# First unit loads, norm weights and tables issued from ScalarE in order of use, and five products of zeros between two feed forwards

## The chip, the cores and the metric

The kernel runs on one core of a Trainium2 chip. TensorE (PE) multiplies matrices, VectorE (DVE), ScalarE (ACT) and GpSimd (POOL) work element by element, and SyncE (SP) issues transfers between HBM and the core's memory; ScalarE and GpSimd can issue transfers too, as instructions in their own streams. The metric is the device time of one execution in microseconds, the median of three runs: 1272.45 us before the change (1271.78 to 1274.7).

## The reference

A block of two layers over 256 tokens of width 1024. Each layer adds half a gated feed forward, a mixer of three attentions, and half a second feed forward to the stream, every one behind a norm of its own; a last norm follows.

```python
def rms_norm(x, gain):
    xf = x.astype(jnp.float32)
    y = xf * lax.rsqrt(jnp.mean(xf * xf, axis=-1, keepdims=True) + NORM_EPS)
    return (y * gain.astype(jnp.float32)).astype(x.dtype)

def swiglu(h, w_gate, w_up, w_down):
    a = jnp.einsum('bsd,df->bsf', h, w_gate)
    u = jnp.einsum('bsd,df->bsf', h, w_up)
    return jnp.einsum('bsf,fd->bsd', jax.nn.silu(a) * u, w_down)
...
    for l in range(DEPTH):
        x = x + 0.5 * swiglu(rms_norm(x, ffn1_norm[l]), ffn1_w_gate[l], ffn1_w_up[l], ffn1_w_down[l])
        x = x + hybrid_mixer(rms_norm(x, mix_norm[l]), w_in[l], q_norm[l], w_uq[l], kv_norm[l], w_ukv[l],
                             w_br_mla[l], w_br_moba[l], w_br_dil[l], w_out[l])
        x = x + 0.5 * swiglu(rms_norm(x, ffn2_norm[l]), ffn2_w_gate[l], ffn2_w_up[l], ffn2_w_down[l])
    return rms_norm(x, final_norm)
```

The feed forward is 2816 wide, all weights are in 32 bits, and every weight is read from HBM once.

## The kernel before

**Products.** Every 32-bit product is made of three (`mm3`, L173): each operand is split into a high part, which ScalarE copies (`high`, L185), and a low part, which VectorE gets by subtraction (`low`, L188). So each block of weights passes through a load, a split on ScalarE and a low part on VectorE before TensorE may use it.

**A feed forward.** The 22 column blocks of 128 of the hidden layer come in three kinds. The first two are made row tile by row tile (`first_block`, L574), with b00 and b01 the gate and up sums of the first and the second 128 tokens; each goes through a silu on ScalarE (L564), a product on VectorE (L568, giving b00_h and b01_h) and transposes on TensorE (b0tp0, b0tp1). Eight single blocks follow (`block`, g2, u2, g3, u3 and so on). The last twelve are two units, each with a gate (G) and an up (U) matrix, made by Strassen's seven products in the order P1, P5, P6, P3, P7, P2, P4. Single blocks and the down products stand between those.

**A unit's quarters.** The weights of a unit's product come as quarters of 128 x 1536 (768 KB), kept in raw buffers a (two), b, c and d (one each). P1 loads a quarter into a, P5 one into b, P6 one into c, P2 one into d; the text calls the first unit's loads G1, G5, G6, G2, and the up matrix's first U1. P5 is made of a + b: VectorE adds G5 into G1 (L351), ScalarE splits the sum. P6 adds G6. GpSimd sends two further quarters that are added in memory while they are loaded.

**Order.** On TensorE, ScalarE and VectorE the instructions stand in the order in which the program writes them. Python plays through the products, counts their time in `clock`, and calls what was deferred (`defer`) when its time has come. Loads are called by `load_some` at a pace; a load's transfer is issued, and the first piece of its split follows at once (`until(total - 1)` in `load`). SyncE is not in that list: its stream holds transfers alone, each waits only for its buffer, so it runs ahead of the other engines until a slot is taken. Split weights lie in a ring of 6656 columns, raw ones in a ring of 4608.

**The start.** SyncE sends x, the first block's weights, then G1, rot and tab (`opened`, tables for the mixer), and only then waits for a slot. Nine products of zeros run first (L1186), while nothing has arrived.

**The norms.** `norm` (L405) is called by the stage before: squares on ScalarE (L429), the sum on VectorE (L435), the root on GpSimd (L436), the scaled rows on VectorE (L452), and `turn` transposes them on TensorE, half a row tile at a time. The weight row is fetched by `gain_tile` (L208) when the first half is done.

Of the kernel before, what the change touches and what calls it, by code (L numbers as in the profile page):

```python
# [110 lines left out]
def block_kernel(ctx: ExitStack, tc: tile.TileContext, a: dict, c: dict, out: bass.AP):  # L111
# [30 lines left out]
    def half_cols(h):  # L142
        return slice(h * 512, (h + 1) * 512)
# [25 lines left out]
    def transpose(o, src, n=P):  # L169
        nc.tensor.transpose(o, src, ident[:n, :n])  # L170
        spend(0.11)

    def mm3(o, st, mv, first, last, again=False):  # L173

        (sh, sl), (mh, ml) = st, mv
        nc.tensor.matmul(o, sh, mh, start=first, stop=False, skip_group_check=again)  # L176
        nc.tensor.matmul(o, sl, mh, start=False, stop=False, skip_group_check=again)  # L177
        nc.tensor.matmul(o, sh, ml, start=False, stop=last, skip_group_check=again)  # L178
        spend(3 * (max(256, o.shape[-1]) / 2400 + 0.003))
        load_some()  # L180
        while later and later[0][0] <= clock[0]:
            heapq.heappop(later)[2]()
# [25 lines left out]
    def gain_tile(src, n, name, tag):  # L208

        g = small.tile([P, n], F32, tag=tag, name=name, bufs=1)  # L210
        nc.sync.dma_start(g, bass.AP(tensor=src.tensor, offset=src.offset, ap=[[0, P], [1, n]]))
        return g

    def x_in(t):
# [98 lines left out]
    def load(j, ring):  # L313
        job = jobs[j]
        name, n = job["name"], job["n"]
        adds = []
        if "unit" in job:
            places, new, add, source, more = job["unit"]
            if new:
                tag, src = new  # L320
                places[tag] = raw_place("raw" + tag, unit_pool[0], 2 if tag == "a" else 1, [P, 4 * UC], f"{name}_r", j)
                nc.sync.dma_start(places[tag][0].rearrange("p (k n) -> p k n", k=4), src)
            for t in {source, *(add or ()), *(more or ())[:1]}:
                for i in places[t][1]:
                    if i in loaded:
                        loaded[i][2]()
                if places[t][1][-1] != j:
                    places[t][1].append(j)
            if more:
                tag, src = more  # L330
                nc.gpsimd.dma_start(places[tag][0].rearrange("p (k n) -> p k n", k=4), src, accum_op=ALU.add)
            raw = places[source][0]
            if add:
                to, other = [places[t][0] for t in add]
                adds = [(to, other)]
        else:
            o, old = take(raws, n, j)
            for i in old:
                loaded[i][2]()
            raw = raws["tile"][:, o:o + n]  # L340
            o = 0
            for w, k0, k1, c0, m in job["runs"]:
                e = o + (k1 - k0) * m
                nc.sync.dma_start(raw[:, o:e].rearrange("p (k n) -> p k n", k=k1 - k0),
                                  w[k0 * P:k1 * P, c0:c0 + m].rearrange("(k p) n -> p k n", p=P))
                o = e
        o, _ = take(rings[ring], n, j)
        hi, lo = [rings[ring][i][:, o:o + n] for i in ("hi", "lo")]
        piece = n // 2 if adds else n if job["whole"] else PIECE
        cuts = [(o, min(n, o + piece)) for o in range(0, n, piece)]  # L350
        todo = [lambda o=o, e=e: nc.vector.tensor_tensor(to[:, o:e], to[:, o:e], other[:, o:e], op=ALU.add)  # L351
                for to, other in adds for o, e in cuts]
        todo += [lambda o=o, e=e: high(hi[:, o:e], raw[:, o:e]) for o, e in cuts]
        todo += [lambda o=o, e=e: low(lo[:, o:e], raw[:, o:e], hi[:, o:e]) for o, e in cuts]
        total = len(todo)

        def until(m):
            while len(todo) > m:
                todo.pop(0)()

        size = piece / 1200 + 0.1
        for m in range(total - 1, -1, -1):
            defer(size * (total - 1 - m), lambda m=m: until(m))
        until(total - 1)
        loaded[j] = hi, lo, lambda: until(0), ring
        return SUM if adds else SPLIT if "unit" in job else PACE * n
# [35 lines left out]
        tl = const.tile([P, KT, S], F32R, tag="xTl", name=f"{name}_Tl")  # L402
        return th, tl

    def norm(name, gain_src, last=None, gain_cols=None):  # L405


        st = {}

        def half_done(t, h):  # L410
            if "g" not in st:
                g = gain_cols is None and gain_tile(gain_src, D, f"{name}_g", "gain")
                st["g"] = g and [g[:, half_cols(i)] for i in range(2)]
                if last is None:
                    nT[name] = transposed(name)
            if h == 0:
                if last is not None:
                    st["xg", t] = row_tile(f"{name}_xg{t}")
                if last is not None and t == 0:
                    st["sq"] = row_tile(f"{name}_sq")  # L420
                st[t] = st["sq"] if last is not None else row_tile(f"{name}_xs{t}"), small.tile([P, 2], F32, tag="ss", name=f"{name}_ss{t}"), \
                    small.tile([P, 1], F32, tag="rstd", name=f"{name}_r{t}")
            defer(0.7, lambda: square(t, h))
            if last is not None:
                nc.vector.tensor_tensor(st["xg", t][:, half_cols(h)], x[t][:, half_cols(h)], st["g"][h], op=ALU.mult)
# [28 lines left out]
            made.add((name, t, "rows"))  # L454

        def turn(t, h):
            tp = tp_bank(f"{name}_tp{t}{h}")
            for k in range(4):
                kk = h * 4 + k
                transpose(tp[:, k, :], st[t][0][:, kk * P:(kk + 1) * P])  # L460
            defer(0.3, lambda: parts_of(t, h, tp))
# [69 lines left out]
    def ffn(name, done, opening=None, opened=None):  # L531
        xTh, xTl = nT[name]
        steps, tail, f_first = ffn_steps()
        with ExitStack() as ctx2:
# [39 lines left out]
            def first_block():  # L574

                pair = hidden(0, 2)
                for t in range(NT):
# [17 lines left out]
                                            made.update((name, "hT", i, t) for i in range(2))))  # L595

                    glu(ab[:, 0, :], ab[:, 1, :], f"{name}_b0{t}", lambda h, t=t: defer(2.5, lambda: turn(t, h)), (name, "h", 0, t))
                if opening:
                    opened()

            single = {}

# [120 lines left out]

            first_block()
            for step in steps:
                if step[0] == "P":
                    unit_product(*step[1:])
                elif step[0] == "B":
                    block(*step[1:])
                else:  # L730
                    for t in range(NT):
                        for h in range(2):
                            down(step[1], t, h)
# [447 lines left out]
    nc.scalar.dma_start(gain_rows, a["ffn1_norm"][0].rearrange("(k p) -> k p", p=P))  # L1181
    nc.scalar.dma_start(ident, c["eye"])
    table(AF.Square)
    heat = acc_bank("heat")
    for _ in range(WARM):
        nc.tensor.matmul(heat[:, :256], zeros[:, :P], zeros, start=True, stop=True)  # L1186
    gain_bank = tp_bank("gain_tp")
    transpose(gain_bank[:, 0, :KT], gain_rows, KT)
    gain_cols = small.tile([P, KT], F32, tag="gc", name="gain_cols", bufs=1)
# [15 lines left out]
        pace[0] = clock[0]  # L1205

    def opened():
        nc.sync.dma_start(rot, c["rot"])
        nc.sync.dma_start(tab, c["tab"])

    def write(t, h, rows_):
        (nc.scalar, nc.sync)[h].dma_start(out[0, rows(t), half_cols(h)], rows_[:, half_cols(h)])
# [2 lines left out]
    for i, (kind, l) in enumerate(layers):  # L1215
        if i + 1 < len(layers):
            k2, l2 = layers[i + 1]
            done = norm(f"{k2}_{l2}", a[norms[k2]][l2])
        else:
            done = norm("last", a["final_norm"], last=write)  # L1220
        if kind == "mx":
# [35 lines left out]
```

## Time and profile before

| what | value |
|---|---|
| median of three runs | 1272.45 us |
| the profiled execution's own time | 1275.12 us |
| its span | 1273.3 us |
| TensorE busy | 1254.1 us (98%) |
| VectorE busy | 913.9 us (72%) |
| ScalarE busy | 748.1 us (59%) |
| GpSimd busy | 55.6 us (4%) |
| read from HBM | 244.85 MB |

The span is the profiled execution from its first to its last instruction; its own time is what the device took for that execution, 1.82 us more. In the rows below PE is TensorE, PEld its weight loads, DVE VectorE, ACT ScalarE, POOL GpSimd and SP SyncE; a q behind an engine's name (SPq, ACTq) marks the issue of a transfer. L185 is line 185 of the kernel. A tile's name has lost its numbers: f_G_r is any gate quarter, w_r, w_h and w_l the rings of raw weights, high and low parts, f_b_s a silu, f_f_b_h a product behind it. What stands in brackets is how long the engine idled ahead of the instruction, and who ended that.

### The profile page before, as it was taken

Reading aid. Unit: us, or ns where it says so; the run is one execution under the profiler, and the core shown is the slowest. Engines: PE = TensorE matmul, PEld = TensorE weight load, DVE = VectorE, ACT = ScalarE, POOL = GpSimd, SP = SyncE. Lnnn points to the kernel's source line nnn. Section 1 sums busy time; section 2 is a strip of 40 time slices with the busy share of each in tenths; the row PEclk is TensorE's granted clock in tenths of the full one; section 3 lists DMA queues with packets and bytes.
Section 4 is the critical chain, followed back from the end, with each engine's and each line's share of the span. In section 5 each row is a group of like instructions: output and inputs, shape, how many; then the busy total and the mean of one; then the engine's idle time right before and its main releaser. Section 6 shows DMA issues by size and latency. Waiting matters only on the chain.

```text
span 1273.3 us, 21204 instructions
## 1 busy us (share of the span) xinstructions
PE 1254.1 (98%) x8287; PEld 1178.7 (93%) x8287; DVE 913.9 (72%) x1359; ACT 748.1 (59%) x1263; POOL 55.6 (4%) x54
## 2 busy tenths in 40 slices
PE   7999999999999999999999999999999999999997
PEld 6999988999999899999889999899999998999996
DVE  5988767765546868887688877667655577788774
ACT  5665646655556456665466565467655554665652
POOL 0000001000000000000000000000000000000000
PEclk8999999999999999999999999999999999999999
DMA  9997856545435688986589985565464466799762
GB/s 301 259 263 207 225 189 172 153 131 145 127 111 169 208 256 221 267 229 174 165 261 261 247 239 151 168 178 154 134 165 115 135 198 199 215 267 242 221 167 79
DMA packets 206308, 247.28 MB, mean 194 GB/s; under 512 B 7160, under 2 KB 190208, under 8 KB 206208
## 3 DMA queue, kind: packets, MB, share of 16 engines
q1 hardware_dynamic: 188864, 220.16, 56.1%
q0 software_dynamic: 16896, 25.17, 12.1%
q8 instruction: 65, 1.06, 0.3%
q10 hardware_dynamic: 448, 0.59, 0.1%
q14 instruction: 35, 0.29, 0.1%
HBM read 244.85 MB, written 1.05 MB: 193 GB/s over the span
## 4 chain that ended last, share of the span: by engine, by line
PE 94%; DVE 3%; ACT 1%; DMA 1%; issue 0%; POOL 0%; POOLq 0%; ACTq 0%; DVEq 0%
PE f_a L178 6%; PE f_a L177 6%; PE f_a L176 6%; PE f_s L176 6%; PE f_s L177 6%; PE f_s L178 6%; PE f_b L177 6%; PE f_b L178 6%; PE f_b L176 6%; PE mx_ogate L176 4%; PE mx_ogate L178 3%; PE mx_ogate L177 3%; PE mx_odqk L176 2%; PE mx_odqk L177 2%; PE mx_odqk L178 2%; PE mx_sbdil L846 1%
## 5 line engine op out<-in xcount | busy, mean ns | idle before, releaser
L188 DVE TENSOR_TENSOR w_l<-w_r,w_h 128x512 fp32r<-128x512 f32 (+1 forms) x484 | 386.4, 824 | 96.7 <-ACT w_h L185 95.0
L185 ACT ACTIVATE w_h<-w_r 128x512 fp32r<-128x512 f32 (+1 forms) x484 | 344.3, 734 | 96.6 <-PE f_a L177 16.8
L176 PE MATMUL f_b<-f_Th,w_h 128*128 128x256 f32 x512 | 144.8, 283 | 0.0
L177 PE MATMUL f_b<-f_Th,w_l 128*128 128x256 f32 x512 | 144.6, 282 | 0.0
L178 PE MATMUL f_b<-f_Tl,w_h 128*128 128x256 f32 x512 | 144.6, 282 | 0.0
L178 PE MATMUL f_a<-w_l,f_hTh 128*128 128x512 f32 x352 | 139.8, 397 | 0.0
L176 PE MATMUL f_a<-w_h,f_hTh 128*128 128x512 f32 x352 | 139.1, 395 | 0.0
L177 PE MATMUL f_a<-w_h,f_hTl 128*128 128x512 f32 x352 | 138.7, 394 | 0.0
L188 DVE TENSOR_TENSOR w_l<-f_U_r,w_h 128x1536 fp32r<-128x1536 f32 (+1 forms) x72 | 100.2, 1399 | 33.1 <-ACT w_h L185 31.9
L185 ACT ACTIVATE w_h<-f_G_r 128x1536 fp32r<-128x1536 f32 (+1 forms) x72 | 86.2, 1199 | 46.4 <-DVE f_G_r L351 18.6
L176 PE MATMUL mx_ogate<-mx_Th,w_h 128*128 128x256 f32 x384 | 113.2, 295 | 0.0
L185 ACT ACTIVATE w_h<-f_U_r 128x1536 fp32r<-128x1536 f32 (+1 forms) x72 | 85.7, 1197 | 41.4 <-issue 14.1
L177 PE MATMUL mx_ogate<-mx_Th,w_l 128*128 128x256 f32 x384 | 108.7, 283 | 0.6 <-DVE w_l L188 0.6
L178 PE MATMUL mx_ogate<-mx_Tl,w_h 128*128 128x256 f32 x384 | 108.6, 283 | 0.0
L188 DVE TENSOR_TENSOR w_l<-f_G_r,w_h 128x1536 fp32r<-128x1536 f32 (+1 forms) x72 | 100.0, 1398 | 10.6 <-ACT w_h L185 10.2
L178 PEld LDWEIGHTS f_b<-f_Tl,w_h 128*128 128x128 f32 x512 | 97.9, 191 | 0.0
L177 PEld LDWEIGHTS f_b<-f_Th,w_l 128*128 128x128 f32 x512 | 97.7, 191 | 0.0
L176 PEld LDWEIGHTS f_b<-f_Th,w_h 128*128 128x128 f32 x512 | 97.6, 191 | 0.0
L176 PE MATMUL f_s<-w_h,f_Sh 128*128 128x384 f32 x256 | 87.3, 341 | 0.0
L178 PE MATMUL f_s<-w_l,f_Sh 128*128 128x384 f32 x256 | 86.7, 339 | 0.0
L177 PE MATMUL f_s<-w_h,f_Sl 128*128 128x384 f32 x256 | 86.6, 338 | 0.0
L178 PEld LDWEIGHTS f_a<-w_l,f_hTh 128*128 128x128 f32 x352 | 66.1, 188 | 15.7
(269 smaller groups left out, 2937.3 us busy)
## 6 DMA issues: line engine op xcount, KB each, us to landing
w_r<-in_ffn_w_down SPq DMA_DIRECT2D x88, 512.0 KB, 4.4
w_r<-in_w_in SPq DMA_DIRECT2D x84, 512.0 KB, 3.9
f_G_r<-in_ffn_w_gate SPq DMA_DIRECT2D x32, 768.0 KB, 7.7
f_U_r<-in_ffn_w_up SPq DMA_DIRECT2D x32, 768.0 KB, 8.6
w_r<-in_ffn_w_gate SPq DMA_DIRECT2D x40, 512.0 KB, 6.1
w_r<-in_ffn_w_up SPq DMA_DIRECT2D x40, 512.0 KB, 6.3
f_G_r<-in_ffn_w_gate POOLq DMA_DIRECT2D x16, 768.0 KB, 8.8
f_U_r<-in_ffn_w_up POOLq DMA_DIRECT2D x16, 768.0 KB, 8.4
```

Source lines behind the costliest of these rows:

```text
L176: nc.tensor.matmul(o, sh, mh, start=first, stop=False, skip_group_check=again)
L177: nc.tensor.matmul(o, sl, mh, start=False, stop=False, skip_group_check=again)
L178: nc.tensor.matmul(o, sh, ml, start=False, stop=last, skip_group_check=again)
L185: nc.scalar.activation(hi, src, AF.Copy)
L188: nc.vector.tensor_tensor(lo, src, hi.bitcast(F32), op=ALU.subtract)
L846: nc.tensor.matmul(o if len(k.shape) == 2 else o.rearrange("p (a b) -> p a b", a=NT), q, k, start=True, stop=True)
```

## The change

Four things are moved or new.

- The first load into each raw buffer (G1, G5, G6, G2, U1, all in feed forward 1 of layer 0) is issued by ScalarE; later ones stay with SyncE.
- The norms' weight rows are issued by ScalarE. Those of width 1024 are asked for 40 us, by the program's own clock, after the norm was set up, no longer at its first half.
- rot and tab are issued by ScalarE ahead of the first unit's product P4 of the gate matrix, no longer behind the first block.
- Where a second feed forward hands over to the next layer's first, five products of zeros stand on TensorE ahead of the second row tile's first transposes. The zeros at the start write a bank of another tag.

```diff
--- before.py
+++ after.py
@@ -170,6 +170,12 @@
         nc.tensor.transpose(o, src, ident[:n, :n])
         spend(0.11)
 
+    def warm(n):
+
+        heat = s_bank("heat")
+        for _ in range(n):
+            nc.tensor.matmul(heat[:, :256], zeros[:, :P], zeros, start=True, stop=True)
+
     def mm3(o, st, mv, first, last, again=False):
 
         (sh, sl), (mh, ml) = st, mv
@@ -208,7 +214,7 @@
     def gain_tile(src, n, name, tag):
 
         g = small.tile([P, n], F32, tag=tag, name=name, bufs=1)
-        nc.sync.dma_start(g, bass.AP(tensor=src.tensor, offset=src.offset, ap=[[0, P], [1, n]]))
+        nc.scalar.dma_start(g, bass.AP(tensor=src.tensor, offset=src.offset, ap=[[0, P], [1, n]]))
         return g
 
     def x_in(t):
@@ -319,7 +325,8 @@
             if new:
                 tag, src = new
                 places[tag] = raw_place("raw" + tag, unit_pool[0], 2 if tag == "a" else 1, [P, 4 * UC], f"{name}_r", j)
-                nc.sync.dma_start(places[tag][0].rearrange("p (k n) -> p k n", k=4), src)
+                first = len(users["raw" + tag]) <= (2 if tag == "a" else 1)
+                (nc.scalar if first else nc.sync).dma_start(places[tag][0].rearrange("p (k n) -> p k n", k=4), src)
             for t in {source, *(add or ()), *(more or ())[:1]}:
                 for i in places[t][1]:
                     if i in loaded:
@@ -402,15 +409,24 @@
         tl = const.tile([P, KT, S], F32R, tag="xTl", name=f"{name}_Tl")
         return th, tl
 
-    def norm(name, gain_src, last=None, gain_cols=None):
+    def norm(name, gain_src, last=None, gain_cols=None, warmed=False):
 
 
         st = {}
 
+        def fetch():
+            if "g" not in st:
+                g = gain_tile(gain_src, D, f"{name}_g", "gain")
+                st["g"] = [g[:, half_cols(i)] for i in range(2)]
+
+        if gain_cols is None:
+            defer(40.0, fetch)
+
         def half_done(t, h):
-            if "g" not in st:
-                g = gain_cols is None and gain_tile(gain_src, D, f"{name}_g", "gain")
-                st["g"] = g and [g[:, half_cols(i)] for i in range(2)]
+            if "begun" not in st:
+                st["begun"] = True
+                if gain_cols is None:
+                    fetch()
                 if last is None:
                     nT[name] = transposed(name)
             if h == 0:
@@ -454,6 +470,8 @@
             made.add((name, t, "rows"))
 
         def turn(t, h):
+            if warmed and t == 1 and h == 0:
+                warm(5)
             tp = tp_bank(f"{name}_tp{t}{h}")
             for k in range(4):
                 kk = h * 4 + k
@@ -595,8 +613,6 @@
                                             made.update((name, "hT", i, t) for i in range(2))))
 
                     glu(ab[:, 0, :], ab[:, 1, :], f"{name}_b0{t}", lambda h, t=t: defer(2.5, lambda: turn(t, h)), (name, "h", 0, t))
-                if opening:
-                    opened()
 
             single = {}
 
@@ -723,6 +739,8 @@
 
             first_block()
             for step in steps:
+                if opening and step == ("P", 0, "G", 4):
+                    opened()
                 if step[0] == "P":
                     unit_product(*step[1:])
                 elif step[0] == "B":
@@ -1181,9 +1199,7 @@
     nc.scalar.dma_start(gain_rows, a["ffn1_norm"][0].rearrange("(k p) -> k p", p=P))
     nc.scalar.dma_start(ident, c["eye"])
     table(AF.Square)
-    heat = acc_bank("heat")
-    for _ in range(WARM):
-        nc.tensor.matmul(heat[:, :256], zeros[:, :P], zeros, start=True, stop=True)
+    warm(WARM)
     gain_bank = tp_bank("gain_tp")
     transpose(gain_bank[:, 0, :KT], gain_rows, KT)
     gain_cols = small.tile([P, KT], F32, tag="gc", name="gain_cols", bufs=1)
@@ -1205,8 +1221,8 @@
         pace[0] = clock[0]
 
     def opened():
-        nc.sync.dma_start(rot, c["rot"])
-        nc.sync.dma_start(tab, c["tab"])
+        nc.scalar.dma_start(rot, c["rot"])
+        nc.scalar.dma_start(tab, c["tab"])
 
     def write(t, h, rows_):
         (nc.scalar, nc.sync)[h].dma_start(out[0, rows(t), half_cols(h)], rows_[:, half_cols(h)])
@@ -1215,7 +1231,7 @@
     for i, (kind, l) in enumerate(layers):
         if i + 1 < len(layers):
             k2, l2 = layers[i + 1]
-            done = norm(f"{k2}_{l2}", a[norms[k2]][l2])
+            done = norm(f"{k2}_{l2}", a[norms[k2]][l2], warmed=kind == "f2")
         else:
             done = norm("last", a["final_norm"], last=write)
         if kind == "mx":
```

ScalarE's stream at the first block of the program, before: the silu of b00, then the split of quarter G1, and the silu of b01 three rows on.

```order
L196 ACT_TABLE_LOAD
L196 ACTIVATE early_79<-mhalf_77 128x2
L564 ACTIVATE f1_0_f1_0_b00_s_246<-f1_0_b00_146 128x256
L185 ACTIVATE w_h_81<-f1_0_G0_1_r_278 128x1536
L185 ACTIVATE w_h_81<-w_r_80 128x1024
L185 ACTIVATE f1_0_hTh0_144<-f1_0_b0tp0_297 128x2x128
L564 ACTIVATE f1_0_f1_0_b01_s_315<-f1_0_b01_248 128x256
L185 ACTIVATE f1_0_Sh_140<-f1_0_xr1_223 128x512
```

The same place now:

```order
L202 ACT_TABLE_LOAD
L202 ACTIVATE early_79<-mhalf_77 128x2
L582 ACTIVATE f1_0_f1_0_b00_s_246<-f1_0_b00_146 128x256
L329 DMA f1_0_G0_1_r_278<-in_ffn1_w_gate 128x4x384
L191 ACTIVATE w_h_81<-f1_0_G0_1_r_278 128x1536
L191 ACTIVATE w_h_81<-w_r_80 128x1024
L191 ACTIVATE f1_0_hTh0_144<-f1_0_b0tp0_297 128x2x128
L582 ACTIVATE f1_0_f1_0_b01_s_315<-f1_0_b01_248 128x256
L329 DMA f1_0_G0_5_r_325<-in_ffn1_w_gate 128x4x384
L191 ACTIVATE f1_0_Sh_140<-f1_0_xr1_223 128x512
```

Two transfers have come in: G1's directly ahead of its split, G5's directly behind the silu of b01.

VectorE's stream at the same place is the one of before, line numbers aside. Here it is now, from the low part of G1 to the second half of the add:

```order
L194 TENSOR_TENSOR w_l_82<-f1_0_G0_1_r_278,w_h_81 128x1536
L194 TENSOR_TENSOR f1_0_hTl0_145<-f1_0_b0tp0_297,f1_0_hTh0_144 128x2x128
L194 TENSOR_TENSOR w_l_82<-w_r_80,w_h_81 128x1024
L650 SCALAR_TENSOR_TENSOR f1_0_xr0_124<-f1_0_xr0_124 128x512
L358 TENSOR_TENSOR f1_0_G0_1_r_278<-f1_0_G0_1_r_278,f1_0_G0_5_r_325 128x768
L194 TENSOR_TENSOR f1_0_Sl_141<-f1_0_xr1_223,f1_0_Sh_140 128x512
L586 TENSOR_TENSOR f1_0_f1_0_b01_h_316<-f1_0_f1_0_b01_s_315,f1_0_b01_248 128x256
L194 TENSOR_TENSOR f1_0_Sl_141<-f1_0_xr0_124,f1_0_Sh_140 128x512
L358 TENSOR_TENSOR f1_0_G0_1_r_278<-f1_0_G0_1_r_278,f1_0_G0_5_r_325 128x768
```

Nothing moved: the first half of the add of G5 stands two rows ahead of b01_h, as before.

SyncE's stream behind the loads of x and of the first block's weights, before (the rows with 8x128 are single blocks, those with 128x1024 down blocks):

```order
L216 DMA x1_73<-in_x 128x512 x2
L344 DMA w_r_80<-in_ffn1_w_up 128x4x256 x2
L322 DMA f1_0_G0_1_r_278<-in_ffn1_w_gate 128x4x384
L1208 DMA rot_75<-c_rot 128x128
L1209 DMA tab_76<-c_tab 128x1792
L344 DMA w_r_80<-in_ffn1_w_gate 128x8x128
L344 DMA w_r_80<-in_ffn1_w_up 128x8x128
L344 DMA w_r_80<-in_ffn1_w_down 128x1024
L322 DMA f1_0_G0_5_r_327<-in_ffn1_w_gate 128x4x384
```

And now:

```order
L222 DMA x1_73<-in_x 128x512 x2
L351 DMA w_r_80<-in_ffn1_w_up 128x4x256 x2
L351 DMA w_r_80<-in_ffn1_w_gate 128x8x128
L351 DMA w_r_80<-in_ffn1_w_up 128x8x128
L351 DMA w_r_80<-in_ffn1_w_down 128x1024
```

G1, rot and tab are gone from ahead of the first single block's load, and G5 from behind the first down block's.

## Rows read from the trace of the kernel before

**Rows 1.** the page: the span, and the chain that ended last by engine

```profile
span 1273.3 us, 21204 instructions
...
PE 94%; DVE 3%; ACT 1%; DMA 1%; issue 0%; POOL 0%; POOLq 0%; ACTq 0%; DVEq 0%
```

**Rows 2.** stretches: length, busy PE, PEld, DVE, ACT, POOL, granted clock, DMA share, GB/s

```profile
24.80:28.80 4.00, 3.63 (x16) 3.44 (x17) 3.29 (x5) 3.31 (x5) 0.00 (x0) 0.59 0.99 323
...
649.60:653.50 3.90, 3.84 (x21) 3.87 (x22) 3.01 (x4) 1.29 (x3) 0.00 (x0) 0.57 1.12 343
```

**Rows 3.** chain of waits in the start: when, how long, what

```profile
14.95 5.62 DMA w_r<-in_ffn_w_gate
```

**Rows 4.** timeline of SyncE's queue: start, length, line, transfer

```profile
6.50 1.35 SPq L322 DMA_DIRECT2D f_G_r<-in_ffn_w_gate  x1
...
9.65 0.53 SPq L1209 DMA_DIRECT2D tab<-c_tab  x1
```

**Rows 5.** the page: DMA issues, KB each, median us to landing

```profile
w_r<-in_w_in SPq DMA_DIRECT2D x84, 512.0 KB, 3.9
```

**Rows 6.** the tile f_G_r (gate units): its loads' landings

```profile
DMA to landing us min/median/max: 4.4/7.9/11.5
```

**Rows 7.** timeline of ScalarE: start, length, line, operation [idle before <-released by]

```profile
28.19 0.37 ACT L564 ACTIVATE f_f_b_s<-f_b 128x256 f32<-128x256 f32 x1
29.32 1.49 ACT L185 ACTIVATE w_h<-f_G_r 128x1536 fp32r<-128x1536 f32 x1 [0.76 <-ACT f_f_b_s L564]
30.74 1.06 ACT L185 ACTIVATE w_h<-w_r 128x1024 fp32r<-128x1024 f32 x1
32.10 0.39 ACT L185 ACTIVATE f_hTh<-f_b0tp 128x256 fp32r<-128x256 f32 x1 [0.31 <-PE f_b0tp L170]
33.17 0.38 ACT L564 ACTIVATE f_f_b_s<-f_b 128x256 f32<-128x256 f32 x1 [0.68 <-PE f_b L178]
...
40.13 0.37 ACT L564 ACTIVATE f_f_b_s<-f_b 128x256 f32<-128x256 f32 x1
```

**Rows 8.** timeline of VectorE, from the add of G5 to the product

```profile
34.72 0.95 DVE L351 TENSOR_TENSOR f_G_r<-f_G_r,f_G_r 128x768 f32<-128x768 f32 x1
...
36.19 0.41 DVE L568 TENSOR_TENSOR f_f_b_h<-f_f_b_s,f_b 128x256 f32<-128x256 f32 x1
```

**Rows 9.** timeline of TensorE in feed forward 1 of layer 0

```profile
37.66 0.38 PE L170 MATMUL f_b0tp<-ident,f_f_b_h 128*128 128x128 f32 x2
...
48.81 0.34 PE L176 MATMUL f_s<-w_h,f_Sh 128*128 128x384 f32 x1
...
63.98 0.34 PE L178 MATMUL f_s<-w_l,f_Th 128*128 128x384 f32 x1
...
73.90 0.34 PE L178 MATMUL f_s<-w_l,f_Th 128*128 128x384 f32 x1
```

**Rows 10.** timeline of ScalarE around the split of quarter G2

```profile
55.20 1.47 ACT L185 ACTIVATE w_h<-f_G_r 128x1536 fp32r<-128x1536 f32 x1
...
59.84 1.49 ACT L185 ACTIVATE w_h<-f_G_r 128x1536 fp32r<-128x1536 f32 x1 [1.81 <-issue]
...
62.18 0.51 ACT L685 ACTIVATE f_G_g<-f_G_g 128x384 f32<-128x384 f32 x1
```

**Rows 11.** timeline of VectorE: the low part of quarter G2

```profile
56.70 1.76 DVE L188 TENSOR_TENSOR w_l<-f_G_r,w_h 128x1536 fp32r<-128x1536 f32 x1
```

**Rows 12.** timeline of TensorE between the two feed forwards

```profile
649.66 0.63 PE L170 MATMUL f_tp<-ident,f_xs 128*128 128x128 f32 x4 [1.83 <-DVE f_xs L452]
```

**Rows 13.** the tile heat (products of zeros): weight loads, ns min/median/max

```profile
L1186 PEld LDWEIGHTS heat<-zeros x18: 190/306/337, 1.2 to 6.7; 128*128 128x128 f32 x18
```

**Rows 14.** timeline of ScalarE: an issue at the start, and a mixer's start

```profile
1.36 0.37 ACTq L1182 DMA_DIRECT2D ident<-c_eye  x1
...
205.58 0.19 ACT L429 ACTIVATION_READ_ACCUMULATOR mx_xs<-x 128x1 f32 x1
```

**Rows 15.** timeline of VectorE at the same mixer's start

```profile
206.26 0.15 DVE L435 SCALAR_TENSOR_TENSOR mx_ss<-mx_ss 128x1 f32<-128x1 f32 x1
```

## The prediction

> **What bounds the kernel now.** I read the page first: the chain of work that ended last is TensorE for 94% of a span of 1273.3 us [rows 1]. So the time is TensorE's work plus the places where it stands still or runs at the lower clock. Then the table by stretches. Twice after the start the granted clock falls to about half: from 24.8 to 28.8 us (0.59) and from 649.6 to 653.5 us (0.57) [rows 2]. What that costs is the missing share: (1 - 0.59) x 4.0 = 1.6 us and (1 - 0.57) x 3.9 = 1.7 us. Those two places, and the starts of the mixers, are where a reordering of loads can gain anything; everywhere else in feed forward 1 of layer 0 TensorE runs without a gap, so a wait put there is paid in full. Last the timelines of the engines around both places.
>
> The chain before 24.8 us hangs on one load: the first-block weights for block 2 ("g2" below), sent at 14.95 and landed 5.62 us later [rows 3]. In SyncE's queue ahead of it stand the first quarter unit (6.50), rot and tab (9.65) [rows 4], 768 + 64 + 896 KB that nobody wants yet.
>
> **The change, part by part.**
>
> Tables and units out of SyncE's queue. The load of g2 finds the transfer engines with 1.7 MB less in front of it. Its issue time stays (it waits for a slot that VectorE frees). I take the landing of a 512 KB load where little else moves, 3.9 us [rows 5], instead of 5.62: all that follows on ScalarE comes 1.7 us earlier (bounds: 0, if the other loads still fill the engines, and little more than 1.7, since 3.9 is from quiet stretches). ScalarE's first silu, which ended at 28.56 (28.19 + 0.37) [rows 7], then ends at 26.85.
>
> Where the units' loads go instead. This is the part that decides. ScalarE now issues the load of quarter G1 right behind that silu, and its very next instruction splits the quarter that has just been asked for. ScalarE works in order, so it stands still for the whole landing, where before the data had been there for 10 us. Behind the split stand the split of the first down block, the high part of the block's first transposes and the second silu; and only behind the second silu is quarter G5 sent. VectorE, whose order is not changed, adds G5 into G1 ahead of the product that TensorE's next transposes wait for (b01_h, then b0tp1). So two landings stand one behind the other between 26.85 and TensorE's transposes, which ran at 37.66 [rows 9]. The rest of this chain, from rows:
> - ScalarE from the split of G1 to the end of the second silu: 1.49 + 1.06 + 0.39 + 0.38 = 3.32, less about 0.1 by which each starts ahead of the end of the one before (30.74 against 30.81): 3.05 us [rows 7].
> - VectorE from the start of the add to the end of b01_h: 34.72 to 36.60, 1.9 us [rows 8].
> - Issue and hand-over, 0.1 us.
> With a landing of L each, the transposes run at 26.85 + 3.05 + 1.9 + 0.1 + 2L = 31.9 + 2L, which is 2L - 5.76 later than before. The 768 KB loads took 4.4 us at the least and 7.9 in the middle [rows 6]. Here little else is under way (SyncE is held by slots, the accumulating loads have not begun), so I take 5.2, near the fast end: +4.6 us. Bounds: 4.4 gives +3.0, 7.9 gives +10.0.
>
> The Trainium skill, "DMA: Bandwidth & Descriptors", section "Anatomy of one DMA", has a fit, 2.0 us plus the bytes over 436 GB/s, stated for loads from GpSimd; it makes 3.8 us of 768 KB, an estimate. By that the two landings would cost 2 x 3.8 - 5.76 = 1.8 us and not 4.6. No 768 KB load of this trace landed that fast (least 4.4), so the sum goes by the rows.
>
> TensorE stands still for some 6 us there. In the two stretches of rows 2 the clock had fallen after far shorter pauses (1.83 us in one piece at 649.66 [rows 12]), so I add one low stretch: +1.6, together +6.2.
>
> The other three first quarters. G6 is now sent behind the silu of block 2, which ended at 40.50 [rows 7], and TensorE came to its product at 48.81 [rows 9]: of the 8.3 us between, a landing of 5.2 leaves 3.1 for an add, a split and a low part of half a unit each, some 0.95 apiece by the add [rows 8]. Just nothing; with a landing of 7.9, 2.4. G2 is sent where its split began, 55.20 [rows 10], now 61.4, again with the split right behind. From the start of the split to the end of its low part it is 3.26 us (55.20 to 56.70 + 1.76) [rows 10, 11]. TensorE's first product that needs the low part stood at 63.98 [rows 9], now 70.2. Accumulating loads and other units are under way by then, so I take L = 6.5: 61.4 + 6.5 + 3.26 = 71.2, a wait of 1.0, together 7.2. U1 follows: from the start of G2's split to the end of the silu ahead of U1's load ScalarE took 55.20 to 62.69, less 1.81 of idling [rows 10], 5.7 us. So U1 is sent at 67.9 + 5.7 = 73.6, lands at 80.1, has its low part at 83.4, and is wanted at 73.90 + 7.2 = 81.1 [rows 9]: +2.3, together 9.5. With 4.4 us a landing both waits are nothing, with 7.9 they are 2.4 and 3.7.
>
> The products of zeros. The second row tile's norm leaves TensorE idle for 1.83 us at 649.66 [rows 12] and the clock falls. Five products stand there now. Nine took 18 instructions from 1.22 to 7.25 us; no row gives their pace at the high clock alone. A weight load of theirs took 190 ns at the least [rows 13], so ten need at least 1.9 us, about the idle time; at the mean of the whole stretch (6.03 / 18 = 0.335) 3.35 us, 1.4 too long. I take an overrun of 0.3, near the lower end since the clock is full as they begin. If the clock stays up the 1.7 us are saved: net -1.4. Bounds: -1.7 and +1.4 (clock falls all the same, long pace).
>
> The norms' weight rows. Most come far ahead of their use and cost ScalarE one issue each, 0.37 us [rows 14], which its pauses for TensorE hide (0.31 and 0.68 in rows 7 alone): nothing. The two rows of the mixers' small norms are now issued between the two squares of the second row tile, on the chain to its transposes: two issues, 0.75 to 1 us, less 0.17 of idling there. The second square's sum, at 205.77 [rows 14], is then there at about 206.55, while VectorE came to it at 206.26 [rows 15]: +0.3 in each of two mixers, +0.6 (bounds 0 and 1.6).
>
> The sum: 9.5 - 1.4 + 0.6 = +8.7 us. The profiled execution took 1275.12 us around its span of 1273.3, which gives 1283.8; the median of the three runs stands 2.67 lower, so the forecast is 1281 us.
>
> **The rivals.**
> - Slower, but little: every landing near the least of 4.4 and no wait at G2 and U1. At the start 3.0 + 1.6, less 1.4, plus 0.6: +3.8, 1276 us. For it: a queue of its own and little traffic. Against it: the middle is 7.9.
> - Slower by far: the loads on ScalarE's queue share the engines with SyncE's, and every landing is at the middle of 7.9. 10.0 + 1.6 + 2.4 (G6) + 2.4 (G2) + 3.7 (U1), less 0.8 for the zeros and the mixers: +19.3, 1292 us. Against it: SyncE's own loads are thinned out by the waits.
> - No change that can be measured, within 0.2% (2.5 us): landings of 4.4 and no fall of the clock: 3.0 - 1.4 + 0.6 = +2.2, 1274.7 us. The fall after only 1.83 us of idling speaks against it.
> - Faster: the waits on ScalarE are covered and only the early crowding goes: 1.7 for g2's load and 1.6 for the low stretch at 24.8, 1.4 for the zeros, less 0.6: -4.1, 1268 us. It decides where two landings fit between 26.85 and 37.66 next to 5.05 us of work, so at a landing under 2.9 us. No 768 KB load came near that. That ScalarE's loads were sent ahead of the instructions they stand behind would do the same, but its first two issues (0.74 and 1.36, then the table load) stand in the order written.
>
> **How the numbers follow.** Forecast 0.55 (own range 1277 to 1287), a little slower 0.18, far slower 0.17, no change 0.06, faster 0.04. Slower by over 0.2% is the sum of the first three, 0.90. The range leaves out the faster and the unchanged case and the far end of the slowest: 1275 to 1290.
>
> **What would show it.** In the profile after: ScalarE idle for 4.5 to 8 us ahead of the first split of G1, released by the load; VectorE's first add of G1 and G5 at about 40 and not 34.7; TensorE idle for some 6 us ahead of the block's second transposes at about 42, then a low clock; pauses of 1 to 3 us ahead of P2 and of U's first product. At the second feed forward pair the clock stays at 1.00 through 650 to 654 (shifted by the loss). I am wrong if ScalarE's gap at G1 is under 3 us, if VectorE's add is not late with it, or if TensorE has no gap in this feed forward.

## The result, and the profile after

The changed kernel took 1286.24 us (median of four runs, 1285.68 to 1292.9) beside 1273.56 for the kernel before (1271.78 to 1274.7): a ratio of 1.0116, 95% interval 1.0099 to 1.0133. In a second comparison (the changed kernel once more, below) the ratio was 1.0123, 1.0104 to 1.0141. So the change costs 12.7 to 15 us. The forecast was 1281 with a range of 1275 to 1290: the direction and the mechanism held, the size was 5 us short.

The profiled execution of the changed kernel took 1292.9 us, its span 1291.1. On the page, the chain that ended last, by engine, to be read beside [rows 1]:

```profile
PE 91%; DVE 3%; DMA 3%; ACT 1%; issue 1%; POOL 0%; POOLq 0%; ACTq 0%; DVEq 0%
```

Loads have come onto the chain. Where TensorE stands is in its timeline (start, duration, engine, line, operation, in brackets the idle time before it and what ended it); the rows answer to [rows 9] and [rows 12]:

```profile
40.96 0.69 PE L170 MATMUL f_b0tp<-ident,f_f_b_h 128*128 128x128 f32 x2 [5.10 <-DVE f_f_b_h L586]
...
52.63 0.39 PE L182 MATMUL f_b<-f_Th,w_h 128*128 128x256 f32 x1 [1.77 <-DVE f_f_b_h L586]
...
74.63 0.58 PE L182 MATMUL f_s<-w_h,f_Th 128*128 128x384 f32 x1 [4.06 <-ACT w_h L191]
...
76.43 0.69 PE L184 MATMUL f_s<-w_l,f_Th 128*128 128x384 f32 x1 [0.89 <-DVE w_l L194]
...
91.03 0.41 PE L182 MATMUL f_s<-w_h,f_Th 128*128 128x384 f32 x1 [2.44 <-DVE f_G_g L700]
...
666.79 2.32 PE L177 MATMUL heat<-zeros 128*128 128x256 f32 x10
668.95 0.60 PE L170 MATMUL f_tp<-ident,f_xs 128*128 128x128 f32 x4
```

The five waits are those ahead of b0tp1, of block 3's product, of P2 (twice: high part, low part) and of U1's product: 14.3 us together. (The last is ended by VectorE's f_G_g, which VectorE reaches at 90.33, behind the low part of U1 at 88.66.) What they go back to is on ScalarE's timeline, beside [rows 7] and [rows 10] (ACTq is an issue by its sequencer):

```profile
19.57 1.58 ACT L191 ACTIVATE w_h<-w_r 128x1024 fp32r<-128x1024 f32 x2 [1.50 <-DMA w_r<-in_ffn_w_gate]
...
25.12 0.39 ACTq L329 DMA_DIRECT2D f_G_r<-in_ffn_w_gate  x1
...
27.16 0.37 ACT L582 ACTIVATE f_f_b_s<-f_b 128x256 f32<-128x256 f32 x1
33.76 1.49 ACT L191 ACTIVATE w_h<-f_G_r 128x1536 fp32r<-128x1536 f32 x1 [6.23 <-DMA f_G_r<-in_ffn_w_gate]
33.95 0.38 ACTq L329 DMA_DIRECT2D f_G_r<-in_ffn_w_gate  x1
...
36.36 0.38 ACT L582 ACTIVATE f_f_b_s<-f_b 128x256 f32<-128x256 f32 x1
...
63.66 0.37 ACTq L329 DMA_DIRECT2D f_G_r<-in_ffn_w_gate  x1
...
73.10 1.48 ACT L191 ACTIVATE w_h<-f_G_r 128x1536 fp32r<-128x1536 f32 x1 [9.03 <-DMA f_G_r<-in_ffn_w_gate]
...
78.01 0.37 ACTq L329 DMA_DIRECT2D f_U_r<-in_ffn_w_up  x1
...
87.14 1.49 ACT L191 ACTIVATE w_h<-f_U_r 128x1536 fp32r<-128x1536 f32 x1 [8.46 <-DMA f_U_r<-in_ffn_w_up]
```

Three times ScalarE asks for a quarter and then stands for 6.2, 9.0 and 8.5 us until it is there. The chain in order of time has the landings of these and of the load of g2, beside [rows 3]:

```profile
15.64 3.90 DMA w_r<-in_ffn_w_gate
...
25.12 8.53 DMA f_G_r<-in_ffn_w_gate
...
43.69 7.51 DMA f_G_r<-in_ffn_w_gate
...
63.66 9.34 DMA f_G_r<-in_ffn_w_gate
...
78.01 9.02 DMA f_U_r<-in_ffn_w_up
```

Last the table by stretches (busy time of PE, PEld, DVE, ACT, POOL with instruction counts, then the granted clock, the share of the transfer engines, GB/s), beside [rows 2]:

```profile
24.00:40.00 16.00, 11.22 (x89) 10.62 (x88) 9.99 (x14) 7.74 (x12) 0.00 (x0) 1.00 0.63 196
40.00:44.00 4.00, 3.04 (x13) 3.04 (x14) 4.00 (x7) 2.90 (x4) 1.30 (x1) 0.58 0.29 117
...
63.60:73.00 9.40, 6.97 (x33) 5.68 (x31) 0.91 (x3) 0.42 (x1) 0.00 (x0) 1.00 1.07 354
...
74.00:82.00 8.00, 6.48 (x24) 5.97 (x25) 6.16 (x5) 4.68 (x6) 0.00 (x0) 0.57 0.67 191
...
90.00:96.00 6.00, 4.97 (x18) 4.67 (x19) 5.72 (x8) 3.52 (x6) 1.29 (x1) 0.72 0.60 200
660.00:673.00 13.00, 13.00 (x95) 12.28 (x94) 9.99 (x16) 8.98 (x18) 1.40 (x1) 1.00 0.94 304
```

Behind three of the waits the clock falls: (1 - 0.58) x 4 + (1 - 0.57) x 8 + (1 - 0.72) x 6 = 6.8 us. At 24.8 and between the feed forwards it does not. Waits and low clock come to 21.1 us; less the two falls of before, 3.3, that is 17.8, and the spans of the two profiles differ by 1291.1 - 1273.3 = 17.8. The sum closes, but not each of its terms is exact: the wait of 0.89 us falls into a low stretch, so it is charged twice in part, and ahead of the first wait TensorE had won 1.8 us (40.96 - 5.10 against 37.66), a little more than the 1.6 of the fall at 24.8.

### The profile page after: what moved, and what is told of

It is laid out like the page before. It is cut to its first block, busy times and chain, and to the rows that moved or that the text cites. A ratio compares the mean times of both kernels' runs of the same rounds, so it can differ in the third digit from the quotient of the medians.

```text
span 1291.1 us, 21227 instructions
## 1 busy us (share of the span) xinstructions
PE 1260.3 (98%) x8297; PEld 1183.1 (92%) x8297; DVE 913.2 (71%) x1359; ACT 747.0 (58%) x1263; POOL 55.7 (4%) x54
## 4 chain that ended last, share of the span: by engine, by line
PE 91%; DVE 3%; DMA 3%; ACT 1%; issue 1%; POOL 0%; POOLq 0%; ACTq 0%; DVEq 0%
PE f_a L184 6%; PE f_a L183 6%; PE f_a L182 6%; PE f_s L182 6%; PE f_s L184 6%; PE f_s L183 6%; PE f_b L182 5%; PE f_b L183 5%; PE f_b L184 5%; PE mx_ogate L182 4%; PE mx_ogate L183 4%; PE mx_ogate L184 4%; DMA f_G_r<-in_ffn_w_gate 2%; PE mx_odqk L182 2%; PE mx_odqk L183 2%; PE mx_odqk L184 2%
```

## The experiments

**One part undone: the units' loads back on SyncE's queue.** Theory A: the whole loss is five loads, each issued just ahead of what wants it. Theory C: the weight rows and tables that ScalarE now issues carry part of it.

```diff
-  (nc.scalar if first else nc.sync).dma_start(places[tag][0]..., src)
+  nc.sync.dma_start(places[tag][0]..., src)
```

> The changed kernel with one part undone: the units' five first loads go back to SyncE's queue; the norms' weight rows and the tables stay on ScalarE, the zeros stay. Theory A (the loss is those five loads alone, each issued from ScalarE just ahead of the split that wants it): TensorE's gaps of the first feed forward (4.4 to 5.1 us at the second transposes, 1.8 at g3, 4.1 at P2, 2.4 at U's first product) are gone, and what is left is the zeros' gain of about 1.5 us and the relief of block 2's load by the tables, 0 to 1: 1270.5 to 1272.5 us beside 1273.5 before. Theory C (the weight rows and tables issued by ScalarE carry part of the loss): 1276 us or more, with gaps of TensorE where ScalarE issues them.

Measured: 1272.13 us beside 1272.93, ratio 0.9996 (0.9987 to 1.0005). The five waits are gone and the load of g2 landed in 3.86 us. Theory A holds, C falls. Of the 1.5 us and more that should have been won, none is measured clear of noise: the interval reaches from 1.7 us faster to 0.6 us slower.

**One part alone: only the units' loads.** The kernel before with the two lines on `first` of the change, and nothing else of it.

> The kernel before with one part of the change alone: the units' five first loads are issued by ScalarE. Theory A: the whole loss comes back, +12.5 to +15 us, about 1287 us, with ScalarE idle for 6 us and more ahead of G1's split and for 8 to 9 ahead of those of G2 and U1. Theory C: less than half of it, 1279 us or less.

Measured: 1288.9 us, ratio 1.0127 (1.0111 to 1.0142): the whole loss. ScalarE stood 4.2, 9.0 and 8.9 us ahead of the splits of G1, G2 and U1, at G1 less than the 6 expected; G1's issue and split on its timeline:

```profile
25.01 0.39 ACTq L323 DMA_DIRECT2D f_G_r<-in_ffn_w_gate  x1
...
31.65 1.49 ACT L185 ACTIVATE w_h<-f_G_r 128x1536 fp32r<-128x1536 f32 x1 [4.23 <-DMA f_G_r<-in_ffn_w_gate]
```

**One load ahead.** Theory A against theory B, that loads from ScalarE's queue are slow wherever they are sent. Each of the five loads is issued by ScalarE where the one before it in order of use was, and G1 where the first block opens. `fetch` takes the buffer and issues the load, `firsts` lists the five:

```diff
-                (nc.scalar if first else nc.sync).dma_start(places[tag][0].rearrange("p (k n) -> p k n", k=4), src)
+                if j in ahead:
+                    places[tag] = ahead.pop(j)
+                else:
+                    places[tag] = fetch(j, nc.sync)
+                if j in firsts()[:-1]:
+                    n_ = firsts()[firsts().index(j) + 1]
+                    ahead[n_] = fetch(n_, nc.scalar)
...
+                            ahead[firsts()[0]] = fetch(firsts()[0], nc.scalar)
```

> The changed kernel with each of the units' five first loads still issued by ScalarE, but one first load earlier in its order: G1 as the first block opens, G5 where G1 was sent, G6 where G5 was, G2 where G6 was, U1 where G2 was. Theory A (what costs is that the wanter stands right behind the load): G1 is there long before its split, G2 and U1 too; G5 still comes a few us late, because it is sent only where G1 was; 1272 to 1277 us. Theory B (ScalarE's queue itself is the slow one, its loads landing in 8 to 9 us wherever they are sent): the waits at G5, G2 and U1 stay for the larger part, 1280 us or more.

Measured: 1274.26 us, ratio 1.0014 (1.0005 to 1.0023): all but some 2 us of the loss is gone. Rows of ScalarE in this kernel: the issue of G1 and its split, the issue of G2 and its split, and the split for P4:

```profile
13.13 0.39 ACTq L327 DMA_DIRECT2D f_G_r<-in_ffn_w_gate  x1
...
28.45 1.49 ACT L191 ACTIVATE w_h<-f_G_r 128x1536 fp32r<-128x1536 f32 x1 [0.30 <-ACT f_f_b_s L597]
...
38.86 0.37 ACTq L327 DMA_DIRECT2D f_G_r<-in_ffn_w_gate  x1
...
55.01 1.49 ACT L191 ACTIVATE w_h<-f_G_r 128x1536 fp32r<-128x1536 f32 x1
...
62.70 1.49 ACT L191 ACTIVATE w_h<-f_G_r 128x1536 fp32r<-128x1536 f32 x1 [4.84 <-DMA f_G_r<-in_ffn_w_gate]
```

None of the five first splits waits for its load, and TensorE's one wait behind the opening is 0.73 us in U. U1's load, sent at 54.51 by the same queue, took 11.0 us to land, more than in the changed kernel, and its split at 65.56 did not stand for it. But this was close: it landed at 65.5, and ScalarE had just stood 4.84 us ahead of P4's split for a quarter that GpSimd had sent at 49.52; TensorE waited for neither. So what decides is not how fast the queue is but how far the load stands from its use. Theory B falls.

**The changed kernel once more.**

> The changed kernel, unchanged, once more: its profiled execution took 1292.9 us and the other three 1285.7 to 1286.6. If the landings of the five loads scatter, its gaps here differ by a few us from those of the first profile, with landings of 6 to 9.5 us, and the time is 1285 to 1293; if the gaps are the same to 0.5 us, the spread is elsewhere.

Measured: 1287.65 us (four runs, 1286.29 to 1290.73). Its profile has a span of 1285.5. TensorE's waits:

```profile
39.03 0.44 PE L170 MATMUL f_b0tp<-ident,f_f_b_h 128*128 128x128 f32 x2 [3.22 <-DVE f_f_b_h L586]
...
69.00 0.69 PE L182 MATMUL f_s<-w_h,f_Th 128*128 128x384 f32 x1 [3.79 <-ACT w_h L191]
...
70.80 0.69 PE L184 MATMUL f_s<-w_l,f_Th 128*128 128x384 f32 x1 [0.79 <-DVE w_l L194]
...
85.51 0.66 PE L182 MATMUL f_s<-w_h,f_Th 128*128 128x384 f32 x1 [3.09 <-DVE f_G_g L700]
```

and the stretches around them:

```profile
38.00:42.00 4.00, 2.97 (x21) 2.98 (x22) 4.00 (x8) 2.83 (x4) 1.23 (x1) 1.00 0.33 122
...
68.00:76.00 8.00, 6.21 (x26) 5.70 (x27) 6.17 (x5) 5.05 (x6) 0.00 (x0) 0.58 0.61 173
...
84.00:90.00 6.00, 4.49 (x17) 4.33 (x18) 5.72 (x7) 3.10 (x6) 1.17 (x1) 0.72 0.58 194
```

The late waits are those of the first profile to within 0.7 us; the first is shorter, block 3's wait is absent, and behind 3.22 us of idling the clock stayed at 1.00. G1's load was sent at 25.07 and its split began at 31.82: 6.75 us, where the first profile had 25.12 to 33.76, 8.64. TensorE's first wait, 3.22 and 5.10, is this time less 3.53 and 3.54. In the run with the units alone it was 3.10 for 6.64, in the run with the early three (below) 6.14 for 9.69: less 3.54 and 3.55. So in four profiles each microsecond of G1's landing beyond the first 3.5 was paid in full.

The sum of waits and low clock, made as for the first profile, is 10.9 + 5.1 - 3.3 = 12.7 us here, and the spans differ by 1285.5 - 1273.3 = 12.2. It charges the low clock too high: the clock had fallen already from 67 to 69 us (0.74), where TensorE still stood.

**The late two, and the early three.** Apart from each other, to price the terms. `first` is narrowed to the tags of G2 and U1, or to those of G1, G5 and G6 (one of the two lines each, remarks added):

```diff
-  first = len(users["raw" + tag]) <= (2 if tag == "a" else 1)
+  first = len(users["raw" + tag]) == (2 if tag == "a" else 1) and tag in "ad"   # late two
+  first = len(users["raw" + tag]) == 1 and tag in "abc"                        # early three
```

> The changed kernel with G1, G5 and G6 back on SyncE's queue; only G2 and U1 are still issued by ScalarE just ahead of their splits. By the prediction's own terms these two cost 1.0 and 2.3, so 1275 to 1276 us after the zeros and tables. By the gaps and low stretches of the changed kernel's profile they cost more: 4.1 + 0.9 + 2.4 of waiting and about 3 of low clock, so 1278 to 1283 us.

> The changed kernel with G2 and U1 back on SyncE's queue; G1, G5 and G6 are still issued by ScalarE just ahead of where they are wanted. The prediction gave this part +6.2 (4.6 of waiting and 1.6 of low clock). From the run with the late two alone (+11.3) and the whole change (+13.7 to +15) it is 3 to 4: 1275 to 1277 us, with a wait of 3 to 5 us ahead of the second transposes, with or without a low stretch behind it. If the parts don't add up, because a delay at the start gives the later two loads more room or less, it is 1280 us or more, or 1273 or less.

Measured: the late two alone 1283.86 us, ratio 1.0090 (1.0076 to 1.0104), +11.4 us; the early three alone 1281.32, ratio 1.0062 (1.0046 to 1.0077), +7.9 us. The first came out above its upper expectation, the second in the branch "don't add up": together they would be 19, and the whole change costs 13 to 15. In the profile of the early three G1 landed later than in any other:

```profile
24.44 0.39 ACTq L329 DMA_DIRECT2D f_G_r<-in_ffn_w_gate  x1
...
34.13 1.48 ACT L191 ACTIVATE w_h<-f_G_r 128x1536 fp32r<-128x1536 f32 x1 [7.28 <-DMA f_G_r<-in_ffn_w_gate]
```

SyncE's timeline of this run shows what was in flight with it, the load of U1:

```profile
22.28 2.22 SPq L329 DMA_DIRECT2D f_U_r<-in_ffn_w_up  x1
```

U1 is sent here 2 us ahead of G1, in the changed kernel at 78.01 by ScalarE. From 30 to 32 us the transfer engines are taken throughout (1.04, 387 GB/s); in the first profile of the changed kernel they are half free then (0.50, 187 GB/s). So moving one load changes what the others share the engines with, and the parts need not add up. That this is the whole of the difference is not shown: in two profiles of the changed kernel itself G1's landing was 8.53 and 6.65.

**Zeros alone.** The kernel before with `warm(5)` ahead of the second row tile's transposes.

> The kernel before with one part of the change alone: five products of zeros ahead of the second row tile's transposes between the two feed forwards. If they hold the clock and fit into the pause: no low stretch at about 650 us, -1.4 to -1.7 us, about 1272 us. Rival (the last of them overruns the pause, or the clock falls a little later all the same): 0 to +1.4, 1273.5 to 1275 us.

Measured: 1273.16 us beside 1272.93, ratio 1.0004 (0.9995 to 1.0013): no gain. In its profile the clock does stay at 1.00 there. So either the zeros cost what they save, or there is mostly nothing to save; hence the next run.

**The kernel before once more.**

> The kernel before, unchanged, profiled once more. In its first profile the granted clock fell at 24.8 and at 649.6 us; the run with zeros alone, the same up to 640 us, showed no fall at 24.8, and had the same median. If the falls belong to the order of the work, both are here again at a granted clock of 0.994. If they come in some executions only, one or both are missing, the clock is 0.995 to 0.997 and the time 1271 to 1274 us.

Measured: 1271.16 us, 4 us under the first profiled execution. The stretches that answer to [rows 2]:

```profile
24.00:30.00 6.00, 5.62 (x45) 5.42 (x46) 5.23 (x9) 5.25 (x8) 0.00 (x0) 1.00 1.13 339
645.00:651.00 6.00, 4.17 (x36) 4.00 (x36) 5.12 (x7) 3.04 (x7) 1.35 (x1) 1.00 1.10 354
```

TensorE idled for 1.82 us between the feed forwards as before, and the clock did not fall. It fell there in two of the four profiles without these zeros and in none of eight with them. The fall at 24.8 was absent here, in the run with zeros alone and in both profiles of the changed kernel, but present in the run one load ahead and in the next one: it comes and goes with the execution. And g2's load landed in 4.18 us, not 5.62, with the tables in front of it.

**Tables alone.** `opened()` moved to G's fourth product, rot and tab issued by ScalarE; the rest as before.

> The kernel before with one part of the change alone: rot and tab are no longer sent by SyncE at the start but by ScalarE at G's last product. The prediction's term: block 2's load lands in 3.9 instead of 5.62 us, all of the opening 1.7 us earlier, so -1 to -2 us. Rival (the units' two loads of 768 KB still fill the transfer engines, the tables were behind the ones that mattered): landing 5.2 us or more, 0.

Measured: 1272.81 us beside 1272.59, ratio 1.0000 (0.9991 to 1.0009), the landing 4.94 us. The landing lies between the two of before, and nothing is won.

**Zeros at the very start.** As the first experiment, with products of zeros in three idle pieces of the opening.

```diff
+  warm(3)     # ahead of the first norm's transposes
+  warm(2)     # ahead of the first product
+  if third[0] == 3: warm(2)     # ahead of the third product with a low part of weights
```

(Shortened, remarks added; `third` counts the products.)

> The changed kernel with the units' first loads back on SyncE's queue, and more products of zeros at the very start, where every profile so far shows a low clock for some 7 us (12 to 20 us) after idle pieces of 1.5, 1.0 and 0.9 to 1.3 us: three, two and two products in those three pieces. If idling is what brings the clock down and TensorE is what the opening waits for, the stretch stays at 1.00 and up to 3.4 us are saved, 1269 to 1271 us. Rival 1 (the opening waits for block 2's load and VectorE, not for TensorE): the clock stays up, but TensorE waits the longer behind it, 0 to -1 us beside the version without these zeros. Rival 2 (the zeros overrun the pieces and delay the transposes): +0.5 to +2 us.

Measured: 1272.13 us beside 1272.79, ratio 0.9994 (0.9985 to 1.0003). A stretch of the opening, and the two rows that show what it waits for then, on TensorE and on ScalarE:

```profile
8.00:20.00 12.00, 9.54 (x59) 7.54 (x59) 8.79 (x18) 6.24 (x13) 1.11 (x2) 1.00 0.99 325
```

```profile
18.72 0.39 PE L189 MATMUL f_b<-w_l,f_Th 128*128 128x256 f32 x1 [1.01 <-DVE w_l L199]
```

```profile
20.11 1.58 ACT L196 ACTIVATE w_h<-w_r 128x1024 fp32r<-128x1024 f32 x2 [2.36 <-DMA w_r<-in_ffn_w_gate]
```

The clock, 0.66 from 10 to 20 us in the second profile of before, is full, and TensorE spends what it gained waiting, here 1.01 us for VectorE; then ScalarE waits 2.36 us for g2's load. The low clock of the opening, where TensorE is not the bound, cost nothing that was measured. No version tried beats the kernel before by more than the measurement can tell.

## Why the prediction was nearly right

- **Two landings one behind the other at the start.** Forecast were transposes at 42.3 behind some 6 us of idling; measured 40.96 and 5.10, in the second profile 39.03 and 3.22. Right in place and nearly in size, but by two errors that cancel. The landings were not 5.2 each but 8.5 and 4.5 (6.7 and 4.5): with these the prediction's 31.9 + 2L puts the transposes at 44.9. The other error: it let each load be issued behind the silu that stands ahead of it in the order. G1's was issued at 25.12 with the silu at 27.16, 1.7 earlier than the forecast's 26.85; G5's 0.19 and not 3.05 us after the start of G1's split, ahead of three activations, the silu at 36.36 among them. That is 4.6 us earlier, of which VectorE, coming to the add 0.6 after the landing, gave some back. The rival "sent ahead of the instructions they stand behind" was half true, and by too little to cover a landing.
- **One low stretch, +1.6.** Right once (0.58 from 40 to 44) and absent in the second profile.
- **G6 "just nothing".** True in the second profile with a landing of 4.7. In the first, 7.51 gave a wait of 1.77 at block 3's product. The prediction had 2.4 for 7.9, but looked for it at P6. It came earlier: on VectorE the add that waits for G6 stands ahead of b02_h, and block 3's product waits for that. Rows of VectorE in the first profile:

```profile
51.28 0.96 DVE L358 TENSOR_TENSOR f_G_r<-f_G_r,f_G_r 128x768 f32<-128x768 f32 x1 [4.50 <-DMA f_G_r<-in_ffn_w_gate]
52.16 0.41 DVE L586 TENSOR_TENSOR f_f_b_h<-f_f_b_s,f_b 128x256 f32<-128x256 f32 x1
```

- **G2 +1.0 and U1 +2.3: here the size was wrong.** Measured 4.06 + 0.89 and 2.44 of waiting, 3.79 + 0.79 and 3.09 in the second profile, and behind them up to 3.4 and 1.7 us of low clock, which the prediction left out although it had charged one behind the first wait. The step that failed is L = 6.5: the landings were 9.34 and 9.02. It had the reason in hand ("accumulating loads and other units are under way by then") and went to the low side of its own middle of 7.9. SyncE's queue in the profile after shows how full it was:

```profile
57.47 0.38 SPq L351 DMA_DIRECT2D w_r<-in_ffn_w_up  x1
59.38 0.37 SPq L329 DMA_DIRECT2D f_U_r<-in_ffn_w_up  x1
60.51 0.34 SPq L351 DMA_DIRECT2D w_r<-in_ffn_w_down  x1
62.18 0.37 SPq L329 DMA_DIRECT2D f_U_r<-in_ffn_w_up  x1
63.32 0.37 SPq L351 DMA_DIRECT2D w_r<-in_ffn_w_gate  x1
```

  Five loads, 3 MB, in the 6 us ahead of G2's issue at 63.66; in the 9.4 us after it the transfer engines were taken throughout (1.07) at 354 GB/s. With 9.34 in place of 6.5 the prediction's own formula gives 61.4 + 9.34 + 3.26 - 70.2 = 3.8 for G2. Over its five loads the forecast had landings of 5.7 in the mean; the first profile had 7.8 and took 1292.9 us, which is the rival "slower by far" (7.9 throughout, 1292), the second 6.9 and 1287.29. That the forecast still came within 5 us of the median owes something to luck: the landings were longer than it took them, and the earlier issue of G1 and G5 gave some of that back.
- **The rule weighed for the landing.** By the fit of the Trainium skill, "DMA: Bandwidth & Descriptors", section "Anatomy of one DMA", which is for loads from GpSimd, 768 KB take 3.8 us, an estimate. None of these loads of ScalarE's landed that fast: 4.3 at the least in any run, and 9.3 behind five others. The measurement decides.
- **The zeros, -1.4: right where the clock fell, nothing in the median.** They do what was said: transposes 2.16 us after the first zeros start, no idling, clock 1.00. The last transposes ahead of the pause, in the first profile of before and in that of the changed kernel:

```profile
640.37 1.04 PE L170 MATMUL f_tp<-ident,f_xs 128*128 128x128 f32 x8
```

```profile
659.49 1.04 PE L170 MATMUL f_tp<-ident,f_xs 128*128 128x128 f32 x8
```

  There the changed kernel is 19.1 us behind, at the end 17.8: 1.3 won. Against the second profile of before, where the clock didn't fall, it is 21.49 behind ahead of the pause (638.00) and 21.63 after it (648.12 and 669.75): 0.14 lost. The fall comes in some executions only (two of four profiles).
- **From the profiled execution to the median, -2.67: partly counted twice.** The execution that the prediction was worked out from had both falls and the late landing of g2; the second profile of before, with neither fall and g2 there after 4.18 us, has a span 3.9 us shorter, and 3.3 of that is the falls' price. So what the prediction took off as the distance to the median it had in part taken off already, with the zeros and with g2's load. The sum for the profiled execution was 1283.8; the second profile of the changed kernel, near the median, took 1287.29, which is 3.5 more, and the 2.67 come on top. No profile was taken of an execution at the median of before, so how the 2.67 split up stays open.
- **Relief of g2's load, -1.7.** The landing came as forecast, 3.90. But 5.62 was the far end of before's (4.18 in the second profile), and the load was sent 0.7 later (15.64 for 14.95), so of the 1.7 about 1.0 was left beside the first profile (there at 19.54 for 20.57); beside the second (19.10) it came 0.4 later.
- **The mixers' small weight rows, +0.6: nothing.** TensorE idled 0.42 us ahead of the first mixer's second transposes, 0.41 before. The two issues (222.96 and 223.32) ran beside the first square (222.95, 0.63 us long), and the second square began 1.20 us after the first, as before. It is the error of the start again: an issue that ran beside the activations was counted into their chain.

Taken together, against the first profile of before, followed product by product: with the last product ahead of P2 TensorE is 6.8 us behind (70.17 for 63.39), and once the clock is back behind U1 it is 19.1 behind (96.38 for 77.27). So G2 and U1 cost 12.3 us where 3.3 were forecast; in the second profile it is 1.4 and 13.4 (64.82 and 90.65), so 12.0. The start cost 40.96 - 37.66 + 1.7 + 1.77 = 6.8 where 6.2 were forecast, but only 1.4 in the second profile, with a shorter landing and no fall of the clock. That is why the median came out 5 us above the forecast and one execution 12.

## What to carry to other kernels

A load that is put into the stream of the engine that uses it must stand at least a whole landing ahead of its use, measured for the time when it is sent: take the landing from loads of that size in that stretch, with what the other queues send at the time, not from the quiet ones. One position earlier gave back nearly everything here, though U1 then landed only as its split came up. And look at more than one profile before a low clock is counted as a loss: one execution's falls may not be the kernel's, and where TensorE was not the bound, in the opening, a full clock won nothing.

## What the runs showed of the hardware

- ScalarE's sequencer issued a load 2.0 us ahead of an activation that stands before it in the program (25.12 and 27.16), and another 0.2 us after the start of an activation four places further up (33.95 and 33.76). In the first profile of the changed kernel three of the five issues came 0.01 to 0.19 us after the start of an activation that had stood for another engine or a load (25.12 behind 25.11, 33.95 behind 33.76, 63.66 behind 63.65), whatever stood between the two in the program. So the order in ScalarE's stream is not the order of issue for loads.
- Loads of 768 KB from the same queue took from 4.5 to 11.0 us within one feed forward (the run one load ahead).
- Idling of 1.8 us was followed by a fall of the clock in two profiles and by none in two others; 3.22 us of idling by none, though 3.10 us in the run with the units alone by one; 3.79 us by a stretch of 8 us at a mean of 0.58.
